# Where the weight sums of the last projection are formed, and where half buffers come from

## The chip, the cores and the metric

The kernel runs on one core of one Trainium2 chip. The core has a matrix engine (PE), a vector engine (DVE), a scalar engine (ACT), a general engine (POOL) and SyncE (SP). In this kernel SP issues all loads from the chip's main memory and some stores, POOL issues the other stores. PE reads its operands from on-chip memory (SBUF) and writes to accumulator banks (PSUM). The metric is the device time of one execution in microseconds (us). A profile is one execution; its row names are those of the profile: "PEld" is PE loading weights, "<-" separates what an instruction writes from what it reads, or a waiting instruction from the one that released it.

## The reference

One step of a decoder with two layers on 1024 prompt tokens and 8 decoded ones, model width 2048, in fp32. Layer A projects to a branch u and a gate, replaces u by differences of trailing means, multiplies by a matrix for each group, gates, and projects back. From its normalised output one shared set of keys and values is made. Layer B is attention over a sliding window of 128 tokens, with a query and a gate projection and an output projection.

```python
z = x @ w_in_a;   u, gate = z[:, :D], z[:, D:]
d = einsum('btgc,gce->btge', multiscale_pool(u) - u, w_grp) * scale
x = layer_norm(ALPHA * x + (d * silu(gate)) @ w_out_a)
k, v = shared_kv(x, w_kv)                        # once
z = x @ w_in_b;   q, gate = rope(z[:, :D]), z[:, D:]
o = window_attention_with_sinks(q, k, v)         # 32 heads of 64, 4 key/value heads
x = layer_norm(ALPHA * x + (o * silu(gate)) @ w_out_b)
```

## The kernel before

**Stages.** The tokens are cut into two chunks, c = 0 (512 tokens) and c = 1 (520 with the decoded ones). The stages run in this order (PHASES): ai0, ai1 (input projection of layer A for each chunk), ao0, ao1 (its output projection), bi0, bi1 (keys, values, queries, gates and the attention of layer B), bo0, bo1 (its output projection). The fifth stage is bi0, the sixth bi1, the seventh bo0. The first few pieces of ai0 and of bi0 are computed plainly; all the rest by seven products.

**Products by seven.** A pair of output tiles (2 x 128 channels) for a chunk is computed by a Strassen scheme: seven products of half size instead of eight. Each product is 8 x 3 matmuls (L687 to L689): the fp32 weight block is split into a high part (cast on ACT, L508) and a low part (subtraction on DVE, L523), and so is the input; three of the four combinations are multiplied. So each product takes one L508 and one L523 of 128 x 1024. PSUM is evicted by ACT and DVE (L626 to L660). The products run in an order written out in the source. `begin` is called before each one: it loads weight blocks for products several ahead (seven for most of the stages in question), casts four ahead and subtracts three ahead. `end` is called after each one: it runs what was put off to this product (events), counts the product, prefetches inputs, takes one step of the `extra` generator and, at intervals, one of a side generator.

**Weight sums.** Of the seven weight blocks of a pair, three are blocks of the matrix and four are sums or differences of blocks. There are three ways to get the sums:

- `first_pair`: when a pair is used for the first time, the blocks are loaded, the four sums are made by DVE in place (L352, 128 x 1024 each) just ahead of their product, and POOL stores each sum for the next use (L354). Five blocks are loaded.
- `next_pair`: the sums were stored before, and all seven blocks are loaded (L288).
- `sum_gen`: the sums of the two output projections are formed ahead, in parts of a quarter of a pair: two loads on SP (L449), three adds on DVE (L456, L460, L461), one store by POOL (L462). For layer B's output weights, `wob`, it is the `extra` generator. It loads a part into a whole slot only if it holds none, if `on` is set and if more than five slots are wholly free; it adds three products later and stores one product after that. `on` is set for one product at the start of bi0 and from the eighth product of bi1 on. `sums` drains the generator at once if a pair's sums are needed and not there.

LATE names pairs of `wob` that `sum_gen` leaves out and that are formed by `first_pair` in bo0, on their first use: pairs 2 and 3 of eight.

**Slots.** All working data share 54 slots of SBUF, managed by `Mem` when the program is built. `full` takes the wholly free slot whose release lies furthest back. `half` takes half a slot: a free half of a slot whose other half is in use if there is one, else a half of a wholly free slot. A clock counts releases; a buffer that a store still reads is released with 10 added to its time. If every free half was released within the last six counts (or was stored) and more than seven slots are wholly free, a wholly free one is opened instead. Whoever writes a newly dealt buffer waits until its former users are done, in the order of its engine's queue.

Places that the prediction speaks of: L929 is DVE's first step of a mean over channels, into a half buffer (`j_steps`, called from `shifted` in bo0); L1986 and L1989 gate an attention head's output and store it; L2096 to L2102 belong to the decoded tokens' attention (`decode`): a normalisation on DVE and then transposes on PE; L898 to L902 form the sums of inputs (`t_ops`).

Of the kernel before, what the change touches and what calls it, by code (L numbers as in the profile page):

```python
# [69 lines left out]
    (6, 3), (7, 2), (7, 1), (6, 4), (7, 3), (7, 4), (4, 5), (4, 6), (5, 5), (5, 6), (6, 5), (6, 6), (7, 5), (7, 6),  # L70
)

LATE = (2, 3)
FORM = (0, 1)
X_KEEP = 5
X_AGE = 3
# [63 lines left out]
class Mem:  # L140
# [22 lines left out]
    def half(self, n=TMAX):  # L163
        fits = lambda i: i < NWIDE or n <= 512
        part = [
            (a if b is None else b, i) for i, (a, b) in enumerate(self.f) if (a is None) != (b is None) and fits(i)
        ]
        if part and min(part)[0] > self.clock - 6 and len(self.whole()) > 7:
            part = []
        i = min(part)[1] if part else min((i for i in self.whole() if fits(i)), key=lambda i: max(self.f[i]))  # L170
        h = 0 if self.f[i][0] is not None else 1
        if not part:
            self.new(i)
        self.f[i][h] = None
        w = TMAX if i < NWIDE else 512
        return Slot(self, i, h, self.t[i][:, h * w : (h + 1) * w])
# [15 lines left out]
class Kern:  # L192
# [187 lines left out]
    def build_stream(self):  # L380
        io = self.io
        w = []
        for kind, c, part in PHASES:
# [33 lines left out]
            else:  # L417
                name = "woa" if kind == "ao" else "wob"
                if (kind, c, part) != PHASES[-1]:
                    prs = [self.next_pair(name, q) for q in range(8)]  # L420
                    if (kind, c) == ("bo", 0):
                        for q in LATE:
                            prs[q] = self.first_pair(name, q)
# [10 lines left out]
    def sum_gen(self, name):  # L434


        W = 256
        qs = [q for q in range(8) if name != "wob" or q not in LATE]
        parts = [(q, slice(W * h, W * h + W)) for q in qs for h in range(4)]
# [144 lines left out]
    def both(self, c, P, Q):  # L584

        runs = [self.seven(c, z0, z1, {6: done}, own=own) for (z0, z1, done), own in (
            (P, self.psW), (Q, self.psW if self.wide else self.psO)
        )]
        for idx in ORDERL:
            for run in runs:  # L590
                run(idx)

    def pair(self, c, z0, z1, done, c11=None):

        run = self.seven(c, z0, z1, {6: done}, c11)
        for idx in ORDER7:
            run(idx)
# [1685 lines left out]
    def run(self):  # L2283
        io = self.io
        self.build_stream()
        self.needs, self.pe, self.summed, self.hurry = [], {}, {}, None
        self.sg, self.qs, self.ao = {}, {}, {}
        self.last = self.turn = self.lock = False
        self.need = {}
        self.shared = False  # L2290
        self.strassen = False
        self.start()

        def add(key, gen):
            self.needs.append((key, gen))
            self.side.append(gen)

        acc, before = {}, False
        for n, (kind, c, part) in enumerate(PHASES):
            self.c, self.ph = c, kind + str(c)  # L2300
            self.strassen = (kind, c, part) not in PLAIN
            self.shared = False
            self.fresh = c == 1 and before and self.strassen
            before = c == 0 and self.strassen
            nxt = n + 1 if n + 1 < len(PHASES) else None
            self.every, self.room = 3, SIDE_KEEP
            if n == 0 or (kind, c) == ("bi", 0) and self.wide:
                self.use_four(kind == "ai")
            elif (kind, c) == ("bo", 0):
                self.at(18, lambda: self.use_four(True))  # L2310

            self.lock = (kind, c) in LOCKED
            self.need = {
                (idx, g): self.i + (2 * n + g - 1 if self.lock else n)
                for n, idx in enumerate(ORDERL if self.lock else ORDER7) for g in range(2)
            } if self.strassen else {}
            self.turn = not self.lock
            self.at(7, lambda: setattr(self, "turn", False))
            self.at(13, lambda: setattr(self, "lock", False))
            if n == 0:  # L2320
                self.at(10, lambda: self.x_begin(1))
                self.at(10, lambda: setattr(self, "turn", True))
            elif (kind, c) == ("ai", 0):
                add(("x", 1, False), self.t_gen(("x", 1)))
                self.room = 99
            elif (kind, c) == ("ai", 1):
                add(("g", 0, False), self.t_gen(("g", 0)))
                self.summed["woa"] = 0
                add("woa", self.sum_gen("woa"))
                self.every = 1.7  # L2330
            elif (kind, c) == ("ao", 0):
                self.every = 2
                self.at(1, lambda: self.nc.sync.dma_start(self.cst[:, K_MP:], io["mask"]))
            elif (kind, c) == ("ao", 1):
                gen = self.ln_gen(0, *acc[0], C_GA, C_BA, self.act["h", 0], self.Td["h", 0])
                self.at(3, lambda gen=gen: add(("h", 0, True), gen))
                self.every = 1.5
            elif (kind, c) == ("bi", 0) and not self.strassen:
                self.summed["wob"] = 0
                self.extra = self.sum_gen("wob")  # L2340
                for k in (4, 5):
                    self.at(k, lambda k=k: setattr(self, "on", k == 4))
                add(("h", 1, False), self.ln_gen(1, *acc[1], C_GA, C_BA, self.act["h", 1], self.Td.get(("h", 1))))

                for k in range(14):
                    self.at(2 * k + 5, lambda: self.side and self.lastO < self.i - 1 and self.side_step())
                self.every, self.room = 1, -20
            elif (kind, c) == ("bi", 1):
                self.at(8, lambda: setattr(self, "on", True))
                self.every, self.room = 1, 0  # L2350
            elif (kind, c) == ("bo", 0):
                self.at(23, lambda: setattr(self, "ahead", (7, 4, 3)))
                self.at(18, lambda: add(("o", 1, False), self.t_gen(("o", 1))))
                self.at(16, lambda: [s.free() for s in self.kv])
                self.rt.free()
            elif (kind, c) == ("bo", 1):
                gen = self.ln_gen(0, *acc[0], C_GB, C_BB, io["y0"], None)
                self.at(3, lambda gen=gen: add("y", gen))
                self.every, self.room = 1.5, 3
            if kind == "ai":  # L2360
                self.phase_ai(c, range(*part), nxt)
            elif kind == "bi":
                self.phase_bi(c, range(*part), nxt)
            else:
                res = self.act["x" if kind == "ao" else "h", c]
                last = (C_GB, C_BB, io["y1"]) if nxt is None else None
                acc[c] = self.phase_out(c, res, nxt, last)
# [141 lines left out]
```

## Time and profile before

| | |
|---|---|
| Median of 3 runs | 2312.7 us (2311.48 to 2317.13) |
| Profiled execution | 2315.52 us, span 2313.7 us |
| Granted clock of PE, mean over the span | 0.997 |
| PE, DVE, ACT busy | 99%, 82%, 60% of the span |
| DMA | 647.77 MB, mean 280 GB/s |
| Stores of `wob` sums by whole blocks (L354) / by parts (L462) | 8 / 24 |

The span runs from the first to the last instruction. A busy share is an average over stages; which stage has room is read from a table of stretches of time, which gives for each one the length, the busy time of each engine with the count of its instructions, the granted clock, the mean busy share of the DMA engines and the rate in GB/s. Waits are listed as waiting instruction, releaser, total, times, longest. In the order of time, the columns are start, length and instruction, and in brackets the idle time of the engine before it and its releaser.

### The profile page before, as it was taken

How to read it: one execution, taken by the hardware profiler on the slowest of the kernel's cores; microseconds unless marked ns; L12 is line 12 of the kernel's file. 1: busy time of each engine (PE TensorE's matmuls, PEld its weight loads, DVE VectorE, ACT ScalarE, POOL GpSimd, SP SyncE). 2: the span in 40 equal slices, each digit the busy share in tenths (PEclk: the TensorE clock that was granted, in tenths of full speed). 3: DMA queues.
4: the chain of work that ended last, by engine and by line, in shares of the span. 5: the costliest groups of instructions: out<-in, count | busy, mean ns of one | idle time of the engine just before them, and what ended most of it. 6: DMA issues, size and time to landing. Idle time of an engine off the chain costs nothing. (4 is left out here: it accounts for less than half of the span.)

```text
span 2313.7 us, 50523 instructions
## 1 busy us (share of the span) xinstructions
PE 2285.5 (99%) x20353; PEld 2214.5 (96%) x20353; DVE 1904.7 (82%) x2413; ACT 1388.2 (60%) x2551; POOL 218.4 (9%) x399
## 2 busy tenths in 40 slices
PE   9999999999999999999999999999999999899998
PEld 8999999999999999999889999999999999899998
DVE  8888889877878878988868888899776777788997
ACT  5544446444546556555567676785676678556665
POOL 0111110010000000000111111100010100010001
PEclk9999999999999999999999999999999999999999
DMA  7779679988889989999777767777776779699894
GB/s 259 266 263 316 228 249 330 314 305 301 301 305 322 338 286 331 320 385 343 236 249 238 243 225 251 268 264 234 242 247 224 250 238 315 210 359 363 297 333 150
DMA packets 252028, 647.77 MB, mean 280 GB/s; under 512 B 27504, under 2 KB 112528, under 8 KB 251792
## 3 DMA queue, kind: packets, MB, share of 16 engines
q1 hardware_dynamic: 208640, 490.20, 63.2%
q0 software_dynamic: 43152, 154.34, 17.3%
q8 instruction: 159, 2.61, 0.5%
q14 instruction: 77, 0.63, 0.1%
HBM read 467.21 MB, written 177.23 MB: 279 GB/s over the span
## 5 line engine op out<-in xcount | busy, mean ns | idle before, releaser
L687 PE MATMUL pD<-m,m 128*128 128x260 f32 (+1 forms) x5088 | 1443.6, 284 | 4.9 <-ACT pD L626 2.2
L689 PE MATMUL pD<-m,m 128*128 128x260 f32 (+1 forms) x5088 | 1436.2, 282 | 6.0 <-DVE m L523 5.7
L688 PE MATMUL pD<-m,m 128*128 128x260 f32 (+1 forms) x5088 | 1436.5, 282 | 0.0
L687 PEld LDWEIGHTS pD<-m,m 128*128 128x128 f32 x5088 | 960.7, 189 | 14.8 <-issue 7.2
L689 PEld LDWEIGHTS pD<-m,m 128*128 128x128 f32 x5088 | 961.4, 189 | 8.0 <-DVE m L523 8.0
L688 PEld LDWEIGHTS pD<-m,m 128*128 128x128 f32 x5088 | 960.8, 189 | 0.5
L523 DVE TENSOR_TENSOR m<-m,m 128x1024 fp32r<-128x1024 f32 x690 | 833.4, 1218 | 94.6 <-ACT m L508 32.2
L508 ACT CAST m<-m 128x1024 fp32r<-128x1024 f32 x690 | 720.6, 1049 | 231.6 <-DVE m L352 118.5
L352 DVE TENSOR_TENSOR m<-m,m 128x1024 f32<-128x1024 f32 x136 | 166.2, 1222 | 15.1 <-DMA m<-in_wia 10.4
L850 DVE TENSOR_TENSOR m<-m,m 128x1024 fp32r<-128x1024 f32 (+1 forms) x118 | 144.0, 1225 | 4.4 <-ACT m L841 3.8
L841 ACT CAST m<-m 128x1024 fp32r<-128x1024 f32 (+1 forms) x118 | 123.4, 1053 | 4.5 <-DMA m<-in_x 2.4
L648 DVE TENSOR_TENSOR m<-pD,m 128x260 f32<-128x260 f32 (+1 forms) x92 | 39.0, 424 | 101.4 <-ACT pD L647 95.3
L660 ACT COPY m<-pD 128x260 f32<-128x260 f32 (+1 forms) x88 | 32.8, 372 | 122.4 <-PE pD L689 121.8
L1935 ACT ACTIVATE m<-m,sm 128x128 f32<-128x128 f32 x256 | 99.3, 392 | 0.0
L632 ACT COPY m<-pD 128x260 f32<-128x260 f32 (+1 forms) x90 | 33.6, 373 | 97.8 <-PE pD L689 93.1
L1184 PE MATMUL pD<-m,m 128*128 128x260 f32 (+1 forms) x528 | 91.5, 323 | 0.0
L715 PE MATMUL pD<-m,m 128*128 128x512 f32 x224 | 89.0, 397 | 0.0
L635 ACT COPY m<-pD 128x260 f32<-128x260 f32 (+1 forms) x92 | 34.4, 374 | 90.8 <-PE pD L689 90.7
L717 PE MATMUL pD<-m,m 128*128 128x512 f32 x224 | 88.2, 394 | 0.0
L716 PE MATMUL pD<-m,m 128*128 128x512 f32 x224 | 88.2, 394 | 0.0
L1184 PEld LDWEIGHTS pD<-m,m 128*128 128x128 f32 x528 | 79.4, 188 | 8.2
L1948 ACT ACTIVATE m<-m,sm 128x128 f32<-128x128 f32 x256 | 81.9, 393 | 2.7 <-DVE sm L1943 2.5
(259 smaller groups left out, 2082.4 us busy)
## 6 DMA issues: line engine op xcount, KB each, us to landing
m<-in_wib SPq DMA_DIRECT2D x132, 512.0 KB
m<-in_wia SPq DMA_DIRECT2D x128, 512.0 KB
m<-swoa SPq DMA_DIRECT2D x64, 512.0 KB
swia<-m POOLq DMA_DIRECT2D x56, 512.0 KB, 4.6
m<-swia SPq DMA_DIRECT2D x56, 512.0 KB
m<-swob SPq DMA_DIRECT2D x56, 512.0 KB
m<-in_wob SPq DMA_DIRECT2D x52, 512.0 KB
m<-in_woa SPq DMA_DIRECT2D x48, 512.0 KB
```

The lines of the kernel that those rows point to most:

```text
L352: self.nc.vector.tensor_add(s[out].a[:, :1024], s[x].a[:, :1024], s[y].a[:, :1024])
L508: self.nc.scalar.copy(hi.r[:, :1024], self.stream[self.cast].src().a[:, :1024])
L523: self.nc.vector.tensor_sub(lo.r[:, :1024], s.src().a[:, :1024], hi.a[:, :1024])
L687: nc.tensor.matmul(ps[:, :TH], wh[:, s], h, start=new and k == 0, stop=False, skip_group_check=on)
L688: nc.tensor.matmul(ps[:, :TH], wh[:, s], l, start=False, stop=False, skip_group_check=on)
L689: nc.tensor.matmul(ps[:, :TH], wl[:, s], h, start=False, stop=k == 7, skip_group_check=on)
L715: nc.tensor.matmul(ps[:], wh[:, s], h, start=par == 0 and k == 0, stop=False)
L716: nc.tensor.matmul(ps[:], wh[:, s], l, start=False, stop=False)
L841: self.nc.scalar.copy(h.r[:, :n], s.a[:, :n])
L850: self.nc.vector.tensor_sub(l.r[:, :n], s.a[:, :n], h.a[:, :n])
L1184: nc.tensor.matmul(ps[:, : cs.stop - cs.start], ws[:, s], d[:, cs], start=f0 and k == 0, stop=l0 and k == 3,)
L1935: nc.scalar.activation(x["s3"][:, i, :], x["s3"][:, i, :], AF.Exp, bias=nm[:, i : i + 1], scale=0.125, accum_out=rs[:, i : i + 1],)
```

## The change

LATE is emptied: all eight pairs of `wob` go through `sum_gen`, and bo0 loads the seven blocks of each pair. In the fifth stage's products by seven, `on` is set from the 20th to the 74th of the 84 products, so that parts can be formed there; before, the first product of the stage and the sixth stage were the only places. And `half` opens a wholly free slot, rather than take a half that was released a moment ago, when more than three slots are wholly free; before, more than seven.

```diff
-LATE = (2, 3)
+LATE = ()
...
-        if part and min(part)[0] > self.clock - 6 and len(self.whole()) > 7:
+        if part and min(part)[0] > self.clock - 6 and len(self.whole()) > 3:
             part = []
...
                 self.every, self.room = 1, -20
+            elif (kind, c) == ("bi", 0):
+                self.at(20, lambda: setattr(self, "on", True))
+                self.at(74, lambda: setattr(self, "on", False))
             elif (kind, c) == ("bi", 1):
```

## The prediction

> **What bounds the kernel now.** I read the page's head first, then the table of stages (busy time of each engine in a stretch), then who waited for whom, for PE alone and for the stretch in which PE waits, and last the order of time on DVE there.
>
> ```profile
> span 2313.7 us, 50523 instructions
> PE 2285.5 (99%) x20353; PEld 2214.5 (96%) x20353; DVE 1904.7 (82%) x2413; ACT 1388.2 (60%) x2551; POOL 218.4 (9%) x399
> ```
> ```profile
> core 0: us, PE busy (x) PEld busy (x) DVE busy (x) ACT busy (x) POOL busy (x), PEclk, DMA share, GB/s
> 52.00:474.00 422.00, 416.84 (x3315) 406.79 (x3314) 361.57 (x452) 214.46 (x320) 45.63 (x94) 1.00 0.82 280
> 1286.00:1466.00 180.00, 180.00 (x2047) 175.72 (x2046) 153.77 (x187) 127.81 (x311) 29.77 (x57) 1.00 0.68 239
> 1475.00:1600.00 125.00, 125.00 (x1326) 122.17 (x1325) 113.53 (x148) 91.55 (x185) 13.55 (x24) 1.00 0.79 269
> 1540.00:1903.00 363.00, 363.00 (x3953) 355.14 (x3952) 274.51 (x388) 242.42 (x573) 33.84 (x52) 1.00 0.72 236
> 1936.00:2128.00 192.00, 181.74 (x1697) 178.21 (x1696) 161.47 (x197) 119.16 (x209) 13.95 (x26) 0.97 0.87 311
> 2002.00:2008.60 6.60, 4.60 (x22) 4.60 (x23) 5.97 (x9) 2.35 (x4) 0.53 (x1) 0.50 0.12 49
> 2088.00:2094.00 6.00, 3.77 (x32) 3.57 (x31) 5.23 (x8) 1.24 (x2) 0.53 (x1) 1.00 1.03 383
> 2094.00:2097.40 3.40, 3.40 (x18) 3.40 (x17) 3.31 (x4) 2.80 (x5) 0.53 (x1) 0.50 1.05 405
> ```
> PE is busy 99% of the span, so PE's matmuls are the bound, and all that a change of weight sums and buffers can touch is the time in which PE waits or runs at a lower clock. That time lies in few places. From 1286 to 1466 us (fifth stage) and from 1540 to 1903 (sixth) PE has no idle time at all. From 1936 to 2128, the stage that projects the attention's output for the first half of the tokens, it is idle for 10.3 of 192 us, and the granted clock is 0.97: it stood at 0.50 twice.
>
> ```profile
> engine line waited for: us in total, times, longest us
> PE pD L689 <- DVE m L523: 5.7, 8, 2.2
> PE pS L2102 <- DVE m L2098: 5.3, 1, 5.3
> ```
> The longest wait of PE in the whole program is the 5.3 us before L2102, a transpose in the attention of the decoded tokens. Who is late there is told by the waits between 1961 and 2046 us and by DVE's order of time:
>
> ```profile
> PE pS L2102 <- DVE m L2098: 5.3, 1, 5.3
> PE pD L687 <- ACT m L660: 1.1, 1, 1.1
> PE pD L689 <- DVE m L523: 0.3, 1, 0.3
> ```
> ```profile
> ACT m L508 <- DVE m L352: 14.4, 4, 7.3
> ```
> ```profile
> 1987.78 3.74 DVE L352 TENSOR_TENSOR m<-m,m 128x1024 f32<-128x1024 f32 x3
> 1991.43 0.68 DVE L1986 SCALAR_TENSOR_TENSOR m<-pS,m 128x512 f32<-128x512 f32 x1
> ...
> 2000.39 0.69 DVE L929 TENSOR_TENSOR m<-m 128x512 f32<-128x512 f32 x1 [4.91 <-DMA o<-m]
> ...
> 2003.66 0.29 DVE L2098 TENSOR_SCALAR m<-m,sm 128x128 f32<-128x128 f32 x1
> ```
> ```profile
> L1989 POOL DMA_DIRECT2D o<-m x1: 544/544/544, 1992.8 to 1992.8; - x1
> ...
> DMA to landing us min/median/max: 7.6/7.6/7.6
> ```
> The reader is to see a chain. Three weight sums of the late pairs (L352) hold DVE for 3.7 us; behind them comes L1986, whose result POOL stores at 1992.8; the store lands 7.6 us later. L929 writes its sum into a half buffer, and the half that it was dealt is the one this store is still reading. DVE works in order, so L929's 4.9 us of waiting also hold up L2098 behind it, for which PE waits. That idle time of PE is followed by 6.6 us at clock 0.50.
>
> **The change, part by part.**
>
> ```profile
> L352 DVE TENSOR_TENSOR m<-m,m x8: 1216/1224/1226, 1987.8 to 2032.3; 128x1024 f32<-128x1024 f32 x8
> ```
> ```profile
> L456 DVE TENSOR_TENSOR m<-m 128x512 f32<-128x512 f32 x56 | 38.3, 684 | 0.0
> ...
> L461 DVE TENSOR_TENSOR m<-m 128x256 f32<-128x256 f32 x56 | 23.8, 425 | 1.9
> ```
> ```profile
> L449 SPq DMA_DIRECT2D m<-in_wob x46: 545/596/1609, 1543.7 to 1881.7; - x46
> ```
> ```profile
> L462 POOL DMA_DIRECT2D swob<-m x24: 711/721/754, 1096.9 to 1903.4; - x24
> ```
> ```profile
> L687 PE MATMUL pD<-m,m 128*128 128x256 f32 x672 | 191.0, 284 | 0.5 <-ACT m L2162 0.5
> ```
> *Pairs 2 and 3 no longer form their sums inside the seventh stage.* There DVE loses eight adds L352, 8 x 1.224 = 9.8 us, and POOL eight stores of 512 KB. SP's loads go from five to seven blocks for each of the two pairs, four more of 512 KB; the stage moves four blocks less in all, at a DMA share of 0.87. On PE's path lie the consequences. ACT's casts no longer stand behind L352 (14.4 us of waiting), so the eviction L660 comes in time: 1.1 us of PE. The wait of L689 for L523, 0.3 us, goes for the same reason.
>
> *Half buffers from whole slots.* L929's half was taken because at most seven slots were wholly free; from now on more than three are enough to leave a half alone that was released a moment ago. The 4.9 us of DVE go if four slots are wholly free then. From L929's start to L2098's end it is 2003.66 + 0.29 - 2000.39 = 3.6 us. Without the wait L929 starts when DVE fell idle, 2000.39 - 4.91 = 1995.5, and L2098 ends at 1999.1; with the three L352 gone some 3.7 us earlier. PE came to L2102 at 2003.95 - 5.3 = 1998.7. So the whole 5.3 us go. With them goes the low clock behind: PE worked 4.6 us at 0.50, which is 2.3 us lost. Next late there is the same L2098 with some 3 us to spare. Bounds of this term: 0, if the half is dealt as before and the store stays as late, to 5.3 + 2.3 = 7.6 us; I take 7.6, since both edits act on this chain. Elsewhere a half now taken from a whole slot leaves one whole slot less for the next full buffer: bounds 0 (PE 363.00 of 363.00 in the sixth stage, where the same slots are short) to 3.9 us for one new wait like that at 2094 (below); I take 0.
>
> The Trainium skill (DMA: Bandwidth & Descriptors, Anatomy of one DMA) gives a store issued by POOL 2.0 us plus bytes/436e3, an estimate of 2.6 us for 256 KB. By that the half would be free before L929 and the second edit worth nothing; the trace has 7.6 us for this very store, so the wait is real here.
>
> *The sums in the fifth stage.* L687 runs eight times for each product by seven, so 672 in 1217.2 to 1500.7 us are 84 products of 3.37 us, and products 20 to 74 last 54 x 3.37 = 182 us, about 1286 to 1467. A part (a quarter of a pair) holds one slot and takes at least four products by the code: at most 13 parts. In the sixth stage 46 loads, 23 parts, ran from 1543.7 to 1903.4, 15.6 us for each: 182/15.6 = 12 parts. I take 12. Each costs DVE 0.684 us for L456 and 0.425 each for L460 and L461, 1.53 us, 18.4 us in all; SP two loads of 0.60; POOL a store of 0.72; 1 MB of DMA. DVE was busy 153.8 of 180 us there and comes to 95%; the DMA traffic goes from 239 GB/s to 239 + 12 MB/182 us = 305 GB/s, less than the 311 of the seventh stage. SP stands still when a part's slot is not yet free, and weight loads queue behind it; they are issued seven products ahead, 24 us. POOL's attention and rotary stores queue behind a part's store, which waits for DVE; they have a product or more in hand. What pays for the DVE work is its waiting:
>
> ```profile
> DVE m L523 <- PE pD L689: 6.1, 5, 1.9
> DVE m L648 <- ACT pD L647: 5.4, 8, 1.0
> DVE m L1962 <- ACT m L1961: 4.2, 7, 0.6
> ```
> These are the longest in 1286 to 1475 us: DVE is ahead and waits for PE to release slots and for ACT; such waits shrink when DVE falls back. Bounds for PE: 0 by the nearest row in load (1475 to 1600: DVE 113.5 of 125 us, 91%, PE without a gap), 2.2 us by the rate of 52 to 474 (5.2 idle in 422, DVE at 86%), 18.4 us if no wait gives way. I take 0.5, near the first. Of all 32 parts one is formed before, 12 here, so that 19 are left for the sixth stage instead of 23, which PE does not notice, as it never waited there.
>
> Sum: 5.3 + 2.3 + 1.1 + 0.3 - 0.5 = 8.5 us less. The profiled execution took 2315.5 us (span 2313.7) and would take 2307.0. The median of the three runs, 2312.7, lies 2.8 us under the profiled execution; the 8.5 us taken off the median give the forecast, 2304.2 us.
>
> **The rivals.**
>
> *A shorter wait stays.* If the half is dealt as before (three whole slots or fewer), only the removed adds act: the store goes out 3.7 us earlier, lands at 1996.7, L2098 ends at 2000.3, PE waits 1.6 us. Then 8.5 - 1.6 = 6.9, or 1.7 us less again if the clock falls: 2305.8 to 2307.5. Whether it falls is told by the rows of 2088 and 2094 above. An idle time of 2.2 us was followed by 3.4 us at 0.50, which is 1.7 us lost; 3.9 in all. The Trainium skill (TensorE: Matmul & The Clock Gate, Why this matters for your kernels) wants gaps of over about 3 us for that; by it a wait of 2.2 us would cost 2.2, not 3.9. The trace disagrees, and its price is used.
>
> *New waits elsewhere.* All slots after the fifth stage's start are dealt anew. The waits that PE has now outside this chain, such as that at 2094, show how one arises: a transfer lands late and DVE queues behind it. One gives 2308.1, two 2312.0. Against it: 543 us in the fifth and sixth stage without one.
>
> *DVE becomes the bound in the fifth stage.* It is at 85% and gets 18.4 us on top. If its 26 us of waiting in 180 are there for reasons that do not give way (casts on ACT that wait for DVE in turn), the stage grows by all of it: 2312.7 + 18.4 - 9.0 = 2322.1, slower. It decides from about 9 us that are not absorbed. For it speaks that DVE was never this full for so long; against it the 91% row.
>
> **How the numbers follow.** 0.3% is 6.9 us: faster lies below 2305.8, slower above 2319.6, which is about what a measurement of this kernel can tell from no change (its three runs spread over 5.7 us). Chances: the forecast 0.55, its own range 2300 to 2307 (the wait at 2094 going too gives 2304.2 - 3.9 = 2300.3), of which 0.07 lies above 2305.8; a shorter wait 0.10, all of it same; new waits 0.17, of which 0.02 for four and more, slower; DVE as the bound 0.18, slower. Faster is then 0.48, same 0.07 + 0.10 + 0.15 = 0.32, slower 0.20. The range is 2299 to 2316: down to the forecast with one more wait gone, up to three new waits (2304.2 + 11.7); DVE's case is left out with the rarest of the others.
>
> **What would show it.** In the changed profile: no wait of L929 for a store; L2102's wait under 1 us; the clock at 1.00 in 1990 to 2030; no L352 for the output weights; 32 part stores L462, a dozen of them between 1286 and 1470 us; DVE about 95% there with PE still without a gap. Wrong would be: PE waiting for L523 or L1962 in the fifth stage, waits over 2 us with the clock at 0.50 in new places, or few parts formed before 1470.

## The result: slower, and the profile after

The changed kernel takes 2327.96 us (median of four runs, 2326.68 to 2333.3); the kernel before took 2313.74 us in the runs beside it (2311.48 to 2317.13). The ratio is 1.0065, with a 95% interval of 1.0051 to 1.008: 0.65% slower, where a gain was forecast. Forecast were 2304.2 us and a range of 2299 to 2316. The profiled execution took 2333.3 us; it is the slowest of the four, so the stages below add up to a little more than the medians differ.

The head of the page after:

```profile
span 2331.5 us, 50594 instructions
PE 2291.8 (98%) x20353; PEld 2219.1 (95%) x20353; DVE 1904.4 (82%) x2429; ACT 1388.0 (60%) x2551; POOL 219.8 (9%) x399
```

The work is the same, PE's 20353 matmuls and DVE's 1904 us. PE is busy 6.3 us longer with the same matmuls, more of which ran at the lower clock, and idle 11.5 us longer. Where, the table of stretches tells. Its columns are the stretch, its length, the busy time of PE, PEld, DVE, ACT and POOL (with instructions), the granted clock, the DMA share and GB/s. The borders after 1345 stand where the subtraction L523 of the same product ends in both kernels: the end of the fifth, sixth and seventh stage. First the kernel before, then after:

```profile
0.00:1345.00 1345.00, 1336.74 (x10759) 1284.91 (x10760) 1116.65 (x1409) 739.07 (x1189) 128.45 (x247) 1.00 0.84 292
1345.00:1497.00 152.00, 152.00 (x1692) 148.66 (x1691) 129.99 (x161) 108.26 (x261) 25.10 (x48) 1.00 0.72 253
1497.00:1935.00 438.00, 437.81 (x4776) 427.91 (x4776) 333.53 (x458) 303.12 (x708) 38.35 (x60) 1.00 0.74 245
1935.00:2126.00 191.00, 180.74 (x1689) 177.21 (x1688) 159.47 (x194) 118.60 (x209) 13.95 (x26) 0.97 0.87 311
```
```profile
0.00:1345.00 1345.00, 1336.67 (x10762) 1285.82 (x10763) 1117.85 (x1416) 737.69 (x1188) 130.77 (x250) 1.00 0.84 294
1345.00:1529.50 184.50, 165.24 (x1707) 158.19 (x1706) 140.53 (x184) 110.48 (x271) 30.34 (x55) 0.95 0.70 244
1529.50:1963.50 434.00, 433.49 (x4743) 423.75 (x4742) 331.92 (x453) 302.88 (x701) 36.90 (x58) 1.00 0.73 244
1963.50:2144.00 180.50, 178.19 (x1706) 175.59 (x1705) 149.33 (x186) 117.71 (x208) 9.70 (x18) 1.00 0.89 313
```

Up to 1345 us the two are alike. The rest of the fifth stage takes 184.5 us for 152; the sixth takes 4 less (the border goes by DVE, which stands less far ahead of PE after the fifth stage, so the two belong together: 28.5 us longer). The seventh stage is 10.5 us shorter. Together with 0.2 at the end that is 17.8, the difference of the spans. The 28.5 us can be read from the two rows together: PE's idle time grows from 0.2 to 19.8 us, nearly all of it in the first of them, and its busy time from 589.8 to 598.7, at a clock of 0.95 in the first. Before, PE was not idle at all in the first row. DVE isn't the one at work: 140.53 of 184.5 us (76%), where it had 129.99 of 152 (86%).

What waits there, on the kernel after, from 1345 to 1500 us, on DVE, then ACT, then PE (in the kernel before neither DVE nor ACT waited for one of these stores there):

```profile
DVE m L523 <- ACT m L635: 12.8, 2, 7.0
DVE m L523 <- DMA swob<-m: 11.7, 3, 4.9
DVE m L523 <- ACT m L508: 7.8, 1, 7.8
```
```profile
ACT m L508 <- DVE m L523: 23.9, 8, 6.1
ACT m L508 <- DMA o<-m: 14.2, 3, 5.4
```
```profile
PE pD L687 <- ACT pD L647: 5.9, 4, 3.4
PE pD L689 <- DVE m L523: 5.1, 4, 1.7
```

The first stall, in the order of time, on POOL, ACT and DVE (start, length, instruction, and in brackets the idle time before it and its releaser):

```profile
1342.05 0.56 POOL L1989 DMA_DIRECT2D o<-m  x1 [0.30 <-ACT m L1916]
...
1354.67 0.72 POOL L462 DMA_DIRECT2D swob<-m  x1 [10.63 <-DVE m L461]
```
```profile
1347.89 1.05 ACT L508 CAST m<-m 128x1024 fp32r<-128x1024 f32 x1 [4.24 <-DMA o<-m]
1348.85 0.36 ACT L635 COPY m<-pD 128x256 f32<-128x256 f32 x1
```
```profile
1349.31 1.22 DVE L523 TENSOR_TENSOR m<-m,m 128x1024 fp32r<-128x1024 f32 x1 [5.82 <-ACT m L635]
...
1359.90 1.23 DVE L523 TENSOR_TENSOR m<-m,m 128x1024 fp32r<-128x1024 f32 x1 [3.30 <-DMA swob<-m]
```

This is the mechanism of L929 again, in another stage. The cast L508 waited for the store issued at 1342.05, so it had been dealt a buffer which that store was still reading, and ACT stood for 4.24 us; the eviction L635 behind it and DVE's L523 came late with it. At 1354.67 POOL stored a part of the output weights' sums, the slot of that part was dealt on to L523, and DVE stood for 3.30 us until the store landed, 5.2 us after its issue. PE ran dry for 3.40 us behind it, up to 1362.5, and the clock stood at 0.50 for 6.8 us from 1361.8.

The seventh stage went as the prediction had it. On the rows of PE's waits from 1964 to 2145 us the 5.3 us of L2102 and the 1.1 of L660 are gone, and the clock is 1.00:

```profile
PE pD L689 <- DVE m L523: 1.5, 1, 1.5
PE pD L687 <- ACT m L641: 0.8, 1, 0.8
```

Ten parts were stored in the fifth stage (twelve were forecast), with these times to landing:

```profile
L462 POOL DMA_DIRECT2D swob<-m x10: 723/726/742, 1304.8 to 1499.6; - x10
...
DMA to landing us min/median/max: 3.3/5.3/9.1
```

### The profile page after: what moved, and what is told of

Read it like the earlier page. It is cut to its first block, busy times and chain, and to the rows that moved or that the text cites. A ratio compares the mean times of both kernels' runs of the same rounds, so it can differ in the third digit from the quotient of the medians.

```text
span 2331.5 us, 50594 instructions
## 1 busy us (share of the span) xinstructions
PE 2291.8 (98%) x20353; PEld 2219.1 (95%) x20353; DVE 1904.4 (82%) x2429; ACT 1388.0 (60%) x2551; POOL 219.8 (9%) x399
## 4 chain that ended last, share of the span: by engine, by line
PE 47%; DVE 4%; issue 4%; DMA 3%; ACT 2%; POOL 0%; DVEq 0%; POOLq 0%; SPq 0%; ACTq 0%
PE pD L687 12%; PE pD L689 12%; PE pD L688 12%; PE pD L715 2%; PE pD L717 2%; PE pD L716 2%; PE pO L1977 2%; PE pS L1899 1%; DVE m L523 1%; DMA m<-swob 1%; PE pS L1952 1%; DMA swob<-m 1%; DVE m L352 1%; ACT m L508 1%; PE pS L1977 0%
## 5 line engine op out<-in xcount | busy, mean ns | idle before, releaser
L687 PE MATMUL pD<-m,m 128*128 128x260 f32 (+1 forms) x5088 | 1444.6, 284 | 15.3 <-ACT pD L647 5.9
L687 PEld LDWEIGHTS pD<-m,m 128*128 128x128 f32 x5088 | 961.9, 189 | 26.4 <-issue 7.5
L523 DVE TENSOR_TENSOR m<-m,m 128x1024 fp32r<-128x1024 f32 x690 | 832.5, 1217 | 121.9 <-ACT m L508 41.7
L508 ACT CAST m<-m 128x1024 fp32r<-128x1024 f32 x690 | 720.0, 1048 | 254.7 <-DVE m L352 109.1
L352 DVE TENSOR_TENSOR m<-m,m 128x1024 f32<-128x1024 f32 x128 | 156.4, 1222 | 16.4 <-DMA m<-in_wia 11.0
L660 ACT COPY m<-pD 128x260 f32<-128x260 f32 (+1 forms) x88 | 32.9, 373 | 127.3 <-PE pD L689 127.3
L635 ACT COPY m<-pD 128x260 f32<-128x260 f32 (+1 forms) x92 | 34.4, 374 | 84.3 <-PE pD L689 84.0
```

Of the source, the lines that this page charges most:

```text
L352: self.nc.vector.tensor_add(s[out].a[:, :1024], s[x].a[:, :1024], s[y].a[:, :1024])
L508: self.nc.scalar.copy(hi.r[:, :1024], self.stream[self.cast].src().a[:, :1024])
L523: self.nc.vector.tensor_sub(lo.r[:, :1024], s.src().a[:, :1024], hi.a[:, :1024])
L687: nc.tensor.matmul(ps[:, :TH], wh[:, s], h, start=new and k == 0, stop=False, skip_group_check=on)
```

## The experiments

Three theories were to be told apart. *DVE's load*: the adds of the parts fill DVE. *The slots*: a part holds a slot, and halves open wholly free slots sooner, so fewer are free and a new buffer is one that a store still reads. *One of the three edits alone* does it. The row under each experiment is that of the fifth stage's stretch from 1286 to 1466 us (before: PE 180.00 of 180, DVE 153.77; after: PE 165.76, DVE 140.84, clock 0.96). Each ratio is to the kernel before, timed beside the run; its medians were 2312.8 to 2313.9 us, so the times of different experiments can be compared to about 1 us.

**The half edit alone.**

```diff
 (the kernel before)
-... and len(self.whole()) > 7:
+... and len(self.whole()) > 3:
```

> Only the edit of the half buffers (more than 3 wholly free slots instead of more than 7); the weight sums as in the kernel before. Theory 'slots' (the parts formed in the fifth stage hold a slot where few are free, so other buffers are dealt slots whose store is still under way): the fifth stage stays without gaps in PE, the wait of L929 in the seventh stage goes, about 5 to 8 us less than before, 2306 to 2309 us. Theory 'halves' (whole slots opened for halves starve the full buffers): the fifth stage gets the new waits, 2320 us or more.

Measured: 2306.22 us (2305.43 to 2307.31), ratio 0.9972 [0.9961, 0.9983].

```profile
1286.00:1466.00 180.00, 180.00 (x2050) 175.70 (x2049) 154.12 (x188) 127.34 (x309) 29.89 (x57) 1.00 0.69 240
```

The half edit alone costs the fifth stage nothing and is worth 6.6 us. In the seventh stage the wait of L2102 goes from 5.3 to 0.6 us, without any of the sums having been moved:

```profile
PE pS L2102 <- DVE m L2098: 0.6, 1, 0.6
```

**Without the window in the fifth stage** (LATE empty, half edit kept).

```diff
 (the changed kernel)
-            elif (kind, c) == ("bi", 0):
-                self.at(20, lambda: setattr(self, "on", True))
-                self.at(74, lambda: setattr(self, "on", False))
```

> The changed kernel without the fifth stage's window: all eight pairs are formed ahead, but from the sixth stage's eighth product on. 'Slots', and likewise 'DVE load' and 'DMA traffic': the fifth stage is as before, the seventh keeps its gain of some 12 us, so about 2302 us; 31 parts at 15.6 us each do not quite fit into the sixth stage, up to 4 us may be lost at its end. 'Halves': the loss stays, 2320 us or more.

Measured: 2310.11 us, 0.9987 [0.9978, 0.9997]. The fifth stage is whole again (PE 180.00 of 180), but the whole is 4 to 8 us slower than expected. The sixth stage does not get through all the parts that are left: of the 31, 24 are stored by its end at 1935.7 us, and seven follow inside the seventh stage. First their stores, then the longest wait of PE behind that border (1935 to 1960 us):

```profile
L462 POOL DMA_DIRECT2D swob<-m x31: 712/721/754, 1559.0 to 2038.5; - x31
```
```profile
PE pD L687 <- ACT pD L626: 3.5, 1, 3.5
```

So the loss in the fifth stage needs the window. Without the window the emptied LATE doesn't pay: with the half edit it is 3.9 us slower than the half edit alone.

**The window, but halves as before.**

```diff
 (the changed kernel)
-... and len(self.whole()) > 3:
+... and len(self.whole()) > 7:
```

> The changed kernel with the old threshold for halves (more than 7). 'Slots': the fifth stage loses about as much as in the changed kernel, 25 to 30 us, and the whole takes 2322 to 2332 us. 'Halves': the fifth stage is as before, 2303 to 2308 us.

Measured: 2310.34 us, 0.999 [0.9981, 1.0], with 12 parts in the fifth stage.

```profile
1286.00:1466.00 180.00, 175.89 (x1992) 170.71 (x1991) 163.45 (x217) 124.14 (x305) 36.88 (x65) 0.99 0.83 287
```

More parts than in the changed kernel, a DVE busier by 10 us than before, and more DMA traffic (287 GB/s; 254 in the changed kernel), and yet PE loses only 4.1 us and some clock there, not 14.2. The time lies between what the two theories gave, nearer to that of the halves. So the parts by themselves, with their adds and their traffic, are a small part of the loss. They are not free of the mechanism: ACT's casts waited 14.7 us in three for stores of input sums (`to`) here.

**One slot held, nothing else** (the kernel before; a slot is taken at the 20th product of the fifth stage and given back at the 74th, and is not used).

```diff
+            elif (kind, c) == ("bi", 0):
+                self.at(20, lambda: setattr(self, "kept", self.mem.full()))
+                self.at(74, lambda: self.kept.free())
```

> The kernel before, and one whole slot is dealt and left unused from the fifth stage's 20th to its 74th product: no added loads, adds or stores. 'Slots': DVE and ACT wait for stores of other buffers, PE gets gaps between 1286 and 1470 us, 10 to 30 us more than before: 2323 to 2343 us. 'DVE load' and 'DMA traffic': no change, 2312 to 2316 us.

Measured: 2312.49 us, 0.9999 [0.999, 1.0009]; PE 179.38 of 180. The expectation that one slot less explains the loss was missed altogether. The half edit is harmless alone, and so is a slot less; that left DVE's load, or the edits acting on each other.

**DVE's load alone** (the kernel before; thirteen times, every fourth product from the 22nd on, three reductions of 512, 256 and 256 columns on DVE, whose results nobody reads).

```diff
+                def more():
+                    for n in (512, 256, 256):
+                        self.nc.vector.tensor_reduce(
+                            self.small(1, 4)[:], self.kv[2].a[:, :n], axis=AX.X, op=ALU.max
+                        )
+                for k in range(22, 74, 4):
+                    self.at(k, more)
```

> The kernel before, and 13 times in the fifth stage's window DVE does three more reductions (512, 256 and 256 columns, results unused), the time of a part's adds, without a slot, a load or a store. Theory 'slots' (parts and opened halves together leave one or two wholly free slots, so that buffers are dealt whose store has just begun): PE keeps working, 2312 to 2318 us. 'DVE load' (DVE at 95% is the bound): 15 us or more on top, 2325 to 2335 us.

Measured: 2312.77 us, 0.9999 [0.9989, 1.0008].

```profile
1286.00:1466.00 180.00, 180.00 (x2048) 175.71 (x2047) 168.24 (x226) 127.35 (x311) 29.77 (x57) 1.00 0.69 239
```

DVE goes to 168.24 of 180 us, 93%, and PE has no gap. These are 14.5 us more work on DVE, of the 18.4 that the prediction counted. DVE's load is not the cause.

**The half edit and one slot held** (the two harmless ones together).

```diff
 (the half edit alone)
+            elif (kind, c) == ("bi", 0):
+                self.at(20, lambda: setattr(self, "kept", self.mem.full()))
+                self.at(74, lambda: self.kept.free())
```

> The kernel before with the edit of the half buffers, and one whole slot dealt and left unused from the fifth stage's 20th to its 74th product; no added work. 'Slots', by the two edits together: the stretch of products 20 to 74 grows by 10 to 30 us, waits of DVE and ACT for stores appear, 2316 to 2336 us against 2306 with the half edit alone. 'Added work' (loads, adds and stores of the parts are needed for the loss): 2304 to 2309 us.

Measured: 2317.96 us, 1.0015 [1.0006, 1.0025]. First its stretch, then its longest waits of DVE and of ACT for stores there (to 1500 us):

```profile
1286.00:1466.00 180.00, 173.66 (x1904) 166.93 (x1902) 145.59 (x179) 120.57 (x296) 28.45 (x54) 1.00 0.66 225
```
```profile
DVE m L523 <- DMA to<-m: 6.4, 1, 6.4
...
ACT m L508 <- DMA o<-m: 9.6, 3, 3.3
```

Here no sum is formed in the fifth stage, no DVE work and no DMA are added, and the stage loses 6.3 us of PE. In that stretch PE loses 0.0 and 0.6 us with either one alone; with both, the whole is 11.7 us slower than with the half edit alone. Neither adds work, and both take wholly free slots, so this much of the loss comes from the supply of slots.

**Loads six products ahead instead of seven**, to give a slot back.

```diff
 (the changed kernel, fifth stage)
                 self.at(20, lambda: setattr(self, "on", True))
+                self.at(20, lambda: setattr(self, "ahead", (6, 4, 3)))
```

> The changed kernel, but weight blocks are loaded six products ahead instead of seven from the fifth stage's 20th product to its 70th, which gives one slot back while all added work stays. 'Slots': most of the loss goes, 2303 to 2313 us. 'Added work': the loss stays, 2322 to 2332 us.

Measured: 2327.22 us, 1.0054 [1.0039, 1.0069]; the gain that was expected did not come. The waits of DVE in the fifth stage:

```profile
DVE m L523 <- DMA swob<-m: 12.4, 3, 5.7
DVE m L352 <- DMA m<-in_wib: 11.1, 4, 4.5
```

This is the range that was given for 'added work'. The waits for part stores stay, and a new one comes: DVE waits 11.1 us for the loads themselves. Since the run changed two things at once, it decides nothing.

**Parts in a slot of their own.** One slot is taken at the 20th product and used for all parts of the fifth stage, one part in seven products, so that it is never dealt to anything else.

```diff
-                s = held[n] = self.mem.full(1024)
+                s = held[n] = self.own or self.mem.full(1024)
...
-            s.free(True)
+            self.stored = s.free(True) if s is not self.own else self.i
...
-(self.on and len(self.mem.whole()) > 5 or hurry)
+(self.on and (self.i - self.stored > 2 if self.own else len(self.mem.whole()) > 5) or hurry)
...
+                def own():
+                    self.own, self.on, self.stored = self.mem.full(), True, self.i
...
+                self.at(20, own)
...
```

> The changed kernel, but in the fifth stage the parts use one slot of their own, dealt at the 20th product and given back after the 74th, so that no other buffer is dealt the slot of a part whose store has just begun. The buffers are dealt there just as in the run with the idle held slot and the new half threshold; the parts' loads, adds and stores (fewer: one part in seven products) come on top. 'Slots': the stretch of products 20 to 74 takes about 193 us as there, against 214 in the changed kernel, and the whole 2305 to 2312 us. 'Added work' (DMA traffic, the queues of SP and POOL): 200 us or more, the whole 2315 us or more.

Measured: 2319.39 us (2317.58 to 2320.89), 1.0027 [1.0017, 1.0037], with 8 parts. Its stretch and its longest waits (L522 and L507 are what was L523 and L508):

```profile
1286.00:1466.00 180.00, 169.73 (x1859) 163.70 (x1858) 147.45 (x193) 115.87 (x287) 31.41 (x57) 0.99 0.73 253
```
```profile
DVE m L522 <- DMA to<-m: 23.3, 3, 8.4
...
ACT m L507 <- DMA o<-m: 10.9, 3, 4.4
```

No wait for a part's store is left among the long ones; those for other stores (`to`, input sums; `o`, attention outputs) stay. It is 8.6 us faster than the changed kernel and 1.4 slower than the idle held slot: the parts' work costs the fifth stage some, 169.73 for 173.66 us of PE, and the seventh gives nearly as much back. By the marks set beforehand that is no clear win for the slots: the total lies in the range given for 'added work', and the stretch of products 20 to 74 took 198 us, between the two. Some of the loss is thus the parts' own work, and the rest goes with the slot that a part gives back under a store; with 8 parts for 10 the two are not cleanly parted.

**The same, with halves as before in the fifth stage.**

```diff
 (parts in a slot of their own)
-... and len(self.whole()) > 3:
+... and len(self.whole()) > (7 if getattr(self.kern, "ph", "") == "bi0" else 3):
```

> The same, with the old threshold for halves in the fifth stage and the new one elsewhere. 'Slots': the stretch takes 184 to 187 us as with the idle held slot alone, the seventh stage keeps 10 to 12 us of gain, 2299 to 2306 us, which would be faster than both kernels. 'Added work': 2310 us or more.

Measured: 2308.87 us, 0.998 [0.997, 0.9989]; PE 176.06 of 180. The time lies between the two ranges (up to 2306, from 2310). With the same 8 parts, taking the half edit back in this one stage is worth 10.5 us. Its longest wait for a store is 15.6 us in three, of the cast for `to`.

**A short window** (products 20 to 40, halves as before in the fifth stage).

```diff
 (the changed kernel)
-... and len(self.whole()) > 3:
+... and len(self.whole()) > (7 if getattr(self.kern, "ph", "") == "bi0" else 3):
...
-                self.at(74, lambda: setattr(self, "on", False))
+                self.at(40, lambda: setattr(self, "on", False))
```

> The changed kernel with the window from the 20th to the 40th product only and the old threshold for halves in the fifth stage (the new one elsewhere). 'Slots': the fifth stage is within 2 us of the kernel before, the seventh keeps 8 to 12 us of its gain, 2300 to 2306 us. 'DVE load' or 'added work': the same less a few us, so this run only tells whether the gain can be had without the loss.

Measured: 2309.72 us, 0.9983 [0.9974, 0.9992], with 5 parts and PE 176.59 of 180. At the border to the seventh stage PE waits 3.0 us for L627 (before: L626), as without a window: five parts seem too few to spare the sixth stage's end. Both expectations were missed: the fifth stage lost 3.4 us of PE where 2 were allowed, and the whole is 4 us slower than the range.

**Other pairs left for the seventh stage** (the half edit alone, and pairs 4 and 5 instead of 2 and 3).

```diff
 (the half edit alone)
-LATE = (2, 3)
+LATE = (4, 5)
```

> The kernel before with the half edit, and the pairs formed late in the seventh stage are 4 and 5 instead of 2 and 3, so that their adds on DVE no longer fall beside the last attention of the decoded tokens. If the place of the late adds is what costs, the seventh stage gains some 3 us over the half edit alone: 2301 to 2305 us. If their number is what costs: 2305 to 2308 us.

Measured: 2308.69 us, 0.9979 [0.997, 0.9989]; PE 180.00 of 180 in the fifth stage, and a wait of L687 for L647 of 2.9 us in the seventh. It is 2.5 us slower than the half edit alone and slower than either range; what that wait comes from was not followed up.

**A guard on the age of slots.** A half opens a slot, and a part is loaded, only if the longest-free slot has been free for a while.

```diff
+    def rested(self, k, d):
+        w = sorted(max(self.f[i]) for i in self.whole())
+        return len(w) > k and w[k] < self.clock - d
...
-... and len(self.whole()) > 3:
+... and len(self.whole()) > 3 and self.rested(0, 3):
...
-(self.on and len(self.mem.whole()) > 5 or hurry)
+(self.on and len(self.mem.whole()) > 5 and self.mem.rested(0, 3) or hurry)
```

> The changed kernel with a guard on age: a half opens a wholly free slot, and a part is loaded, only if the wholly free slot whose release lies furthest back was released at least four counts ago (a buffer under a store counts ten later). Counted in the program, 11 instead of 25 whole buffers of the 20th to 74th product are then dealt while a store has just begun to read them, and 8 instead of 11 parts are formed in the fifth stage. If those deals are the cause, the loss of about 25 us in that stretch falls with their number, to 11/25 of it, about 11 us: with 2303 us for the change without the loss (the half edit alone took 2306.2, and the seventh stage gains 3.4 more), 2314 us, between 2308 and 2319. If instead the work of the parts is the cost, it falls only to 8/11 of it, about 18 us: 2321 us. If neither, the time stays at 2328.

Measured: 2322.49 us (2321.1 to 2323.95), 1.004 [1.0026, 1.0054], with 7 parts in the fifth stage. Its stretch, and DVE's longest waits for stores there (L527 is what was L523):

```profile
1286.00:1466.00 180.00, 169.52 (x1858) 163.59 (x1857) 148.61 (x194) 115.68 (x286) 32.45 (x59) 0.99 0.72 250
```
```profile
DVE m L527 <- DMA to<-m: 7.2, 1, 7.2
...
DVE m L527 <- DMA swob<-m: 4.2, 1, 4.2
```

5.5 us are won back, not the 14 expected, and the time is nearer to what the count of parts gave (2321). That count can't be the measure either: twelve parts with the old halves took 2310.3 us, and no part at all with a held slot and the new halves 2318.0. So the loss does not grow in proportion to the buffers dealt early; what would decide is which of these deals falls on a cast or a subtraction for which PE has nothing in hand; no run shows that by itself. How large the loss gets for a given order of deals stays open.

Side by side, what was held in the fifth stage, with either rule for halves. Each cell has the median, then from the profiled execution the end of the sixth stage (of its last L523) and the waits of DVE and ACT for stores from 1286 to 1500 us, all in us:

| fifth stage | halves: more than 7 | halves: more than 3 |
|---|---|---|
| nothing | 2312.7 / 1934.8 / 0 (kernel before) | 2306.2 / 1933.5 / 0 |
| idle slot held | 2312.5 / 1932.6 / 2.8 | 2318.0 / 1943.4 / 16.0 |
| parts in one own slot | 2308.9 / 1942.1 / 15.6 (new halves in the other stages) | 2319.4 / 1949.5 / 34.2 |
| parts in dealt slots | 2310.3 / 1939.5 / 15.2 | 2328.0 / 1963.4 / 25.9 (the changed kernel) |

The end of the sixth stage is the fairer measure, since the lower two rows have LATE emptied, which shortens the seventh stage; but it is that of one execution each, and those of one kernel spread by 2 to 7 us. On the left it moves by -2 to +7 us, on the right by 10, 16 and 30: the edits act on each other, and that is shown. The right column also splits the loss roughly: 10 us with a slot gone and no work, 6 more with the parts' work in a slot of their own, 14 more when their slots go back into the deal (and ten parts are formed instead of eight). Waits for stores come when a slot is gone: none in the first row, 2.8 to 34.2 us below it. Their sum doesn't give the loss, though: 34.2 us cost less than 25.9.

## Why the prediction was wrong

*The chain of L929 and L2102* (5.3 + 2.3 us) and *the casts behind L352* (1.1 + 0.3): right. 9.0 us were forecast, the seventh stage is 10.5 us shorter. One thing was not drawn from the prediction's own numbers: for the chain the half edit alone suffices (2306.2 us). It had L2098 ending at 1999.1 without the wait and PE coming at 1998.7, which leaves 0.4 us; 0.6 were measured. The moved sums shorten the seventh stage further, by some 3 us (from last L523 to last L523 184.0 us with the half edit alone, 180.6 with both), while the window that goes with them costs, together with the half edit, ten times that in the fifth.

*"Elsewhere a half now taken from a whole slot leaves one whole slot less for the next full buffer: bounds 0 ... to 3.9 us ...; I take 0", and "The sums in the fifth stage ... I take 0.5"*: here it failed. Each was costed against the kernel before, as if the other were not there, and each alone is cheap (180.00 us of PE out of 180 with the half edit; 179.38 with a held slot; 175.89 with the parts and the old halves, which is already some 4 us against 0.5). Both take from the same supply of wholly free slots. Together they cost 28.5 us in the profiled execution, where 0.5 were forecast. The cost of a part was listed as DVE's adds, SP's loads, POOL's store and 1 MB of traffic; the slot that it holds, and that goes back into the deal with a store still on it, was named only as something SP might wait for. It was DVE and ACT that waited. That slots short of supply make the loss is shown for its first 10 us, where no work was added; how much of the rest is work and how much slots is known only roughly.

*The bounds of the sums* (0, 2.2, 18.4 us) all came from DVE's load. None was made from the row that had the mechanism, L929's 4.9 us of waiting for a store: three waits of DVE and three of ACT like it, 11.7 + 14.2 us, are what the fifth stage got.

*The rivals.* "New waits elsewhere" named the mechanism (a transfer lands late and DVE queues behind it) but priced it at one or two waits, 2308 to 2312 us, gave four and more of them 0.02, and used the 543 us without a wait against it. A stage without a gap says nothing of how near it is to one. "DVE becomes the bound" gave 2322 us, nearer to the result by luck, through a mechanism that was not there: DVE fell to 78% (140.84 of 180) instead of going to 95%, and at 93% with the slots untouched PE lost nothing.

*What was to be seen*: no wait of L929, L2102 under 1 us, the clock at 1.00 in the seventh stage and 32 part stores all came; DVE at 95% in the fifth stage with PE without a gap did not. PE's waits for L523 and L1962 in the fifth stage and clock 0.50 in new places, which the prediction had named as the signs of its failure, came too.

The best kernel of these is the half edit alone, 2306.22 us, 0.9972 [0.9961, 0.9983] of the kernel before.

## What to carry to other kernels

Where a change has two edits that draw on one pool of buffers, price them together: ask which buffer the next instruction gets, and whether a store is still reading it, and take the price of being wrong from the waits for a store that the trace has already. A stage in which the bounding engine has no gap is not a stage with room; a trial that takes one buffer away with no work added shows how near the edge it is. And run the edits one by one: here one of three alone was faster than every combination that was run (the emptied LATE was never run alone).

## What the runs showed of the hardware

*The clock falls after less idle time than one long gap.* Rows of the kernel after; the clock is the third column from the end:

```profile
1351.60:1355.00 3.40, 2.06 (x18) 1.85 (x16) 3.26 (x7) 1.55 (x8) 0.33 (x1) 1.00 0.89 261
1382.30:1385.70 3.40, 1.19 (x10) 0.98 (x9) 3.37 (x3) 2.15 (x3) 0.00 (x0) 1.00 0.83 295
1385.70:1389.10 3.40, 3.40 (x18) 3.40 (x17) 3.33 (x6) 2.12 (x11) 0.00 (x0) 0.50 0.09 36
1409.60:1413.00 3.40, 1.81 (x13) 1.41 (x13) 1.79 (x2) 2.26 (x3) 0.00 (x0) 1.00 0.44 145
1413.00:1416.40 3.40, 3.40 (x18) 3.40 (x18) 3.30 (x6) 1.06 (x6) 0.00 (x0) 0.50 0.09 27
1443.70:1447.10 3.40, 2.60 (x23) 2.36 (x21) 1.49 (x2) 0.23 (x1) 0.00 (x0) 1.00 0.22 89
1447.10:1450.50 3.40, 2.25 (x19) 2.26 (x20) 3.15 (x4) 3.40 (x10) 0.55 (x1) 1.00 0.30 123
```

One gap of 2.2 us (second row) and 1.6 us in two gaps (fourth) were each followed by 3.4 us at 0.50; a single gap of 1.9 us, from 1446.3 to 1448.2, was not. The Trainium skill (TensorE: Matmul & The Clock Gate, Part 1: The HAM clock gate) tells of a free-running window of 3413 ns; the lengths of 3.4 and 6.8 us at 0.50 agree with that. So do their places: in the fifth stage the clock fell at 1361.8, 1385.7, 1413.0 and 1471.0 us, which lie 7, 8 and 17 times 3.41 us apart. The rows above are cut at that spacing. A border of it at 1447.1 splits the gap of 1.9 us into 0.8 and 1.1. In this stage the four stretches of 3.41 us with 1.6 us of idle time or more were followed by the low clock. Of the stretches that ran at the full clock, none with 1.3 us (first row) or less was; where between the two it turns no row shows. The advice of the Trainium skill on the same page (Why this matters for your kernels), no gaps over about 3 us, is too mild for these rows.

*Stores of 512 KB and of 256 KB landed about equally late.* The ten part stores (512 KB) of the fifth stage took 5.3 us in the median from issue to landing, with 3.3 to 9.1 between the fastest and the slowest; the ten stores L1989 (256 KB) there took 5.1:

```profile
L1989 POOL DMA_DIRECT2D o<-m x10: 544/547/564, 1230.5 to 1493.1; - x10
...
DMA to landing us min/median/max: 2.5/5.1/8.1
```

So a buffer that was dealt here right after its store was issued could be kept back for some 5 us, at most 9, with either size; the single waits for these stores were up to 5.4 us.
